# First loads in a fixed order and sixteen operand differences on GpSimd, in a two-layer encoder kernel

## The chip, the core and the metric

The kernel runs on one core of one Trainium2 chip. Its engines are TensorE (PE in the profile; PEld is its weight load), VectorE (DVE), ScalarE (ACT), GpSimd (POOL) and SyncE (SP). SP only issues DMAs; ACT issues a few beside its own work. The metric is the device time of one execution in microseconds, as a median of several runs.

## What is computed

A two-layer encoder trunk over two groups of 512 tokens of width 1024, with the same weights for both groups.

```python
def trunk(x, ...):
    for i in range(DEPTH):                       # DEPTH = 2
        h = rms_norm(x, norm_g[i], NORM_EPS)
        if i % N_MIXERS == 0:
            x = x + diff_attention(h, da_w_in[j], ..., da_w_out[j], lambda_init)
        else:
            x = x + bidir_retention(h, ret_w_in[j], ..., ret_w_out[j])
    return rms_norm(x, final_norm_g, NORM_EPS)

def diff_attention(h, w_in, ...):
    proj = h @ w_in                              # (512, 1024) @ (1024, 8192)
    q, k, v, gate = jnp.split(proj, ...)
    # rotary q and k, two softmaxes a head, their difference times v,
    # a norm a head, times silu(gate)
    return o @ w_out                             # (512, 2048) @ (2048, 1024)
```

The second layer has the same shape of projections (1024 to 6144 columns), with retention in both directions in place of the softmaxes. `reference` calls `trunk` once for `x_prompt` and once for `x_sample`.

## The kernel before

**Precision.** Each float32 operand of a large product is split into a high part, rounded to the matmul's fast float type, and a low part, the remainder. A product of two such operands takes three matmuls (`PASSES`). ACT makes the high part (`hi_of`, line 419), DVE the low part (`lo_of`, line 422), which reads the source and the high part and so two tensors of SBUF when the source lies there.

**Input projections.** They go by a scheme of seven products in place of eight for a two-by-two block of operands (the two groups of tokens on one side, halves of weight columns and of the inner dimension on the other). Per 256 weight columns there is a `Unit`; its seven products are called P1 to P7 and each needs one activation operand: B11, B21, T1, T2, B22, T3 and T4 (`B_OF`). These seven are made once per layer, in four pieces (k = 0 to 3) of 128 x 512 with a high and a low part, by `make_b` (line 467). It turns the normed tokens by transposes through PSUM, scales them by the norm's gain, and combines them: `h11` and `h21` are the first group's halves, `t` is first the second group's half less `h11` (T1) and then the other half less that (`scaled`, line 482; T2). The third piece's operand is `t - h11` (T3) and the fourth's `h21 - t` (T4). Both differences go through `sub` (line 494), one DVE `tensor_tensor` of 128 x 512, four for T3 and four for T4 in each layer; then `split` makes their high and low parts.

**Start.** Twenty short matmuls on zeros (`warm_up(10)`, line 1061) run first on PE. `x_norm` (line 1064) squares a row tile of 128 tokens on ACT, takes the root on POOL and scales the tile on ACT or DVE. For the first group the tiles are turned one at a time as they come (`turns`, line 1106), and `first_piece` (line 1089) makes B11's pieces in two halves of 256 tokens. `gains` (line 440) turns the norm gains, loaded as rows, into columns; it needs the identity matrix, as all transposes do. In the first two units P1 is issued in small steps: `prep` splits unit 0's first weight tile in four parts (lines 607 to 613), and `product` issues each of the two P1s as eight steps of three matmuls on 256 columns, by half and k (lines 650 to 661). All other products are one step of twelve matmuls on 512 columns (line 633).

**Order.** The program is not issued as it is written. Each operation is put into a `Plan` with its engine, an estimate of its time, and what it reads and writes. `Plan.arrange` then simulates the engines and DMA queues and lists the operations in the order in which it would start them: for PE close to the written order, for the other engines by how soon PE needs the result. It does so three times, each time with PE's simulated times from before, and the shortest list is issued. Each engine then works through its list in order. The planner knows no contention between DVE and POOL. `plan.first` (line 82), where it is set, makes every load that is put in afterwards wait, in the list, for one earlier operation to have been placed.

**Loads.** `dma` (line 412) issues on SP unless an engine is named. The identity (line 426), the three gain rows (line 438) and the first group's row tile 1 (line 1033) go on ACT's queue; the other row tiles and all weights on SP's.

Of the kernel before, what the change touches and what calls it, by code (L numbers as in the profile page):

```python
# [16 lines left out]
S = 512  # L17
# [238 lines left out]
def trunk_kernel(  # L256
# [167 lines left out]

    ident = const([P, P], "ident")
    dma(lambda: ident.t, lambda: ident_in, [], [ident], 64, nc.scalar)
    mhalf = const([P, NT], "mhalf")
    dve(4, lambda: nc.vector.memset(mhalf.t, -0.5), [], [mhalf])
    minus1 = const([P, 1], "minus1")
# [4 lines left out]
    for i, (lo, hi, src) in enumerate((  # L434
            (0, 16, norm_g.rearrange("l (k p) -> (l k) p", p=P)),
            (16, 18, da_subln_g.rearrange("l (k p) -> (l k) p", p=P)),
            (18, 20, ret_subln_g.rearrange("l (k p) -> (l k) p", p=P)))):
        dma(lambda lo=lo, hi=hi: rows[lo:hi, :], lambda src=src: src, [], [(rows, i)], 8, nc.scalar)

    def gains(behind):  # L440

# [25 lines left out]
    def make_b(layer, source):  # L467


        def parts(name, k, hi, lo, r):  # L470
            t = slot(B_SLOT[name] + k, [P, 2, S])
            hi(lambda: t[:, 0, :], r, [(t, 0)])
            lo(lambda: t[:, 1, :], lambda: t[:, 0, :], r + [(t, 0)], [(t, 1)])
            Bop[name, k] = t

        def split(name, k, src, key):
            parts(name, k, lambda out, r, w: hi_of(S, out, src, r, w),
                  lambda out, hi, r, w: lo_of(S, out, src, hi, r, w), [key])

        def scaled(out, ps, scale, less, r, w):  # L480

            dve(S, lambda: nc.vector.scalar_tensor_tensor(  # L482
                out(), ps.t, scale(), less(), op0=ALU.mult, op1=ALU.subtract), [ps, gcol] + r, w)

        def split_bank(name, k, ps, scale):
            parts(name, k, lambda out, r, w: plan.op(
                "ACT", 0.1 + 0.00092 * S,
                lambda: nc.scalar.activation(out(), ps.t, AF.Copy, scale=scale()), r + [gcol], w),
                lambda out, hi, r, w: scaled(out, ps, scale, lambda: hi().bitcast(F32), r[1:], w), [ps])

        def copy(out, ps, scale, late=()):
            evac(S, out[0], lambda: ps.t, scale, [ps, gcol, *late], [out[1]])

        def sub(out, a, b):

            dve(S, lambda: nc.vector.tensor_tensor(out[0](), a[0](), b[0](), op=ALU.subtract),
                [a[1], b[1]], [out[1]])

        def half(t, i):
            return (lambda: t[:, i, :]), (t, i)  # L500

        def whole(t):
            return (lambda: t.t), t

        two = [os_t(F32, "h") for _ in range(3)]
        h11 = [half(two[k // 2], k % 2) for k in range(4)]
        h21 = [whole(m_t("h")) for _ in range(4)]
        for name, h, k0 in (("B11", h11, 0), ("B21", h21, 4)):
            for k in range(4):
                if (name, k) in Bop and layer == 0:  # L510
                    for n in range(2):
                        ps, src = turned[n][k // 2], slice(k % 2 * 256, k % 2 * 256 + 256)
                        here = slice(n * 256, n * 256 + 256)
                        evac(256, lambda h=h[k][0], here=here: h()[:, here], lambda ps=ps, src=src: ps[:, src],
                             lambda k=k: gain(0, k), [ps, gcol, (Bop[name, k], (1, n))], [h[k][1]])
                    yield
                    continue
                bank_ = source(0, k0 + k)
                if layer == 0:
                    split_bank(name, k, *bank_)  # L520
                copy(h[k], *bank_, [(Bop[name, k], 1)] if layer == 0 else [])
                if not (layer == 0):
                    split(name, k, *h[k])
                yield
        t = [whole(e_t("h")), whole(e_t("h")), half(two[2], 0), half(two[2], 1)]
        for k in range(4):
            ps, scale = source(1, k)
            scaled(t[k][0], ps, scale, h11[k][0], [h11[k][1]], [t[k][1]])
            split("T1", k, *t[k])
            yield  # L530
        for k in range(4):
            ps, scale = source(1, 4 + k)
            scaled(t[k][0], ps, scale, t[k][0], [t[k][1]], [t[k][1]])
            split_bank("B22", k, ps, scale)
            split("T2", k, *t[k])
            sub(h11[k], t[k], h11[k])
            split("T3", k, *h11[k])
            yield
        for k in range(4):
            sub(h21[k], h21[k], t[k])  # L540
            split("T4", k, *h21[k])
            yield


    class Unit:
# [32 lines left out]
        def prep(self, op):  # L578
            x = self.take
            n = 256 if self.wide else P  # L580

            def combine(a, b, fn):
                t = st_t([P, 4, n])
                out = ((lambda: self.like(t.t)), t)
                dve(4 * n, lambda: nc.vector.tensor_tensor(out[0](), a[0](), b[0](), op=fn), [a[1], b[1]], [t])
                return out
            if op == "P1":
                src = x(0, 0)
            elif op == "P2":
                src = x(0, 1)  # L590
            elif op == "P4":
                src = x(1, 1)
            elif op == "P5":
                src = self.s[1] = combine(x(1, 0), x(1, 1), ALU.add)
            elif op == "P6":
                src = self.s[2] = combine(self.s[1], x(0, 0), ALU.subtract)
            elif op == "P3":
                src = combine(x(0, 1), self.s[2], ALU.subtract)
            else:
                src = combine(x(0, 0), x(1, 0), ALU.subtract)  # L600
            if self.wide:
                a, b = ws_t([P, 4, n], True), ws_t([P, 4, n], True)
                hi, lo = ((lambda: a.t), a), ((lambda: b.t), b)
            else:
                s = ws_t([P, 2, 4, n])
                hi, lo = ((lambda: s[:, 0]), (s, 0)), ((lambda: s[:, 1]), (s, 1))
            if op == "P1" and self is first_units[0]:
                for k in range(4):
                    hi_of(n, lambda k=k: self.like(hi[0]())[:, k], lambda k=k: src[0]()[:, k], [src[1]], [(s, (0, k))])
                    lo_of(n, lambda k=k: self.like(lo[0]())[:, k], lambda k=k: src[0]()[:, k],  # L610
                          lambda k=k: self.like(hi[0]())[:, k], [src[1], (s, (0, k))], [(s, (1, k))])
                self.ops[op] = (hi, lo)
                return
            hi_of(4 * n, lambda: self.like(hi[0]()), src[0], [src[1]], [hi[1]])
            lo_of(4 * n, lambda: self.like(lo[0]()), src[0], lambda: self.like(hi[0]()), [src[1], hi[1]], [lo[1]])
            self.ops[op] = (hi, lo)
            if op == "P2" and self.early is not None:
                self.early, self.x = None, {}

        def product(self, op):  # L620
# [27 lines left out]
            if not self.wide:  # L648
                ps = self.banks[which][0]
                if op == "P1" and self in first_units[:2]:  # L650
                    def piece(k, half):
                        here = slice(half * 256, half * 256 + 256)
                        for i, (u, v) in enumerate(PASSES):
                            nc.tensor.matmul(
                                ps[:, here], a[u][0]()[:, k, :], bt[k][:, v, here], start=(half + k + i == 0),
                                stop=(k == 3 and i == 2), skip_group_check=True)
                    for half in range(2):
                        for k in range(4):
                            pe(0.36, lambda k=k, half=half: piece(k, half),
                               ([(a[0][1][0], (n, k)) for n in range(2)] if self is first_units[0] else reads[:2])  # L660
                               + [(bt[k], (0, half)), (bt[k], (1, half))], [(ps, (k, half))])
                else:
                    pe(2.79, lambda: pair(ps), reads, [ps])
                return
# [365 lines left out]
    for g in range(NG):  # L1030
        for t in range(NT):
            x = xnat[g, t] = slot(20 + 4 * g + t, [P, D], F32)
            dma(lambda x=x: x.t, lambda g=g, t=t: xs[g][0, t * P:(t + 1) * P, :], [], [x], 512,
            nc.scalar if (g, t) == (0, 1) else None, 2.0 if g else 0.6)
            if g == 0:
                plan.first = len(plan.ops) - 1
        if g == 0:
# [566 lines left out]
```

## Time and profile before

| | |
|---|---|
| median of 3 runs | 1807.33 us (1807.0 to 1808.09) |
| profiled execution | 1806.59 us, span 1804.5 us |
| granted clock of TensorE, mean | 0.999 |
| DMA | 328.81 MB, mean 182 GB/s |
| ACT, of the span | 50% |
| POOL, of the span | 9%, x315 |

A line number in the profile is one of the kernel's; where a helper records an operation, it is the helper's (419 and 422 for all splits, 496 for all sixteen differences). `out<-in` gives the buffers: ws, raw and st hold weights, arena and b the activation operands, e, m, os and c are working buffers in SBUF, pad holds columns, and pj, sc, o and tp are banks of PSUM. The profiled execution's own time contains some 2.1 us around the span.

### The profile page before, as it was taken

What the parts mean: (1) busy time and instruction counts of PE and PEld (TensorE: products, weight loads), DVE (VectorE), ACT (ScalarE), POOL (GpSimd) and SP (SyncE); (2) the same over time, 40 slices, a digit from 0 to 9 for tenths busy, and PEclk for the clock granted to TensorE, in tenths of its full rate; (3) what the DMA queues carried; (4) which work ended last, traced back from release to release, by engine and by line L of the source; (5) the groups of instructions that cost most, each with busy time, mean ns of one, the idle gap of its engine ahead of it and who ended that gap; (6) DMA issues with size and microseconds to landing.
All of it is one profiled execution on the core that took longest, in us unless ns stands there. A gap on an engine that the chain in (4) does not pass through costs nothing.

```text
span 1804.5 us, 27874 instructions
## 1 busy us (share of the span) xinstructions
PE 1789.8 (99%) x10333; PEld 1566.1 (87%) x10333; DVE 1479.1 (82%) x2344; ACT 895.9 (50%) x1865; POOL 169.2 (9%) x315
## 2 busy tenths in 40 slices
PE   9999999999999999999999999999999999999998
PEld 7889889898988888888888888898989998888887
DVE  8967878778699888888888897787887967888887
ACT  8753344443343565555454866444444455444446
POOL 1000000000000022322322200000000000111113
PEclk9999999999999999999999999999999999999999
DMA  6444455655545594444554524464647459664652
GB/s 218 134 134 135 158 150 166 199 164 155 177 124 187 204 344 179 172 162 156 179 205 140 195 68 147 140 210 156 207 151 231 144 182 399 262 232 185 228 216 94
DMA packets 162767, 328.81 MB, mean 182 GB/s; under 512 B 12724, under 2 KB 76872, under 8 KB 162632
## 3 DMA queue, kind: packets, MB, share of 16 engines
q1 hardware_dynamic: 162160, 326.18, 53.5%
q8 instruction: 81, 1.33, 0.3%
q10 hardware_dynamic: 472, 0.86, 0.1%
q14 instruction: 54, 0.44, 0.1%
HBM read 209.55 MB, written 117.44 MB: 181 GB/s over the span
## 4 chain that ended last, share of the span: by engine, by line
PE 93%; DVE 3%; ACT 1%; DMA 1%; issue 0%; POOL 0%; SPq 0%; ACTq 0%; POOLq 0%; DVEq 0%
PE pj L633 20%; PE pj L934 19%; PE sc L633 11%; PE pj L643 10%; PE o L633 8%; PE o L1251 5%; PE sc L643 5%; PE sc L1186 5%; PE o L1429 2%; PE o L643 2%; PE tp L1231 1%; PE sc L1385 1%; PE tp L1409 1%; PE o L1437 1%; DVE ws L422 1%; DMA raw<-in_da_w_out_dram 1%
## 5 line engine op out<-in xcount | busy, mean ns | idle before, releaser
L934 PE MATMUL pj<-ws,arena 128*128 128x512 f32 x1542 | 389.8, 396 | 0.0
L934 PEld LDWEIGHTS pj<-ws,arena 128*128 128x128 f32 x1542 | 277.3, 188 | 50.6
L633 PE MATMUL pj<-b,ws 128*128 128x512 f32 x1080 | 263.2, 390 | 0.0
L633 PEld LDWEIGHTS pj<-b,ws 128*128 128x128 f32 x1080 | 201.3, 188 | 41.7 <-DVE e L687 0.5
L939 DVE SCALAR_TENSOR_TENSOR b<-pj,pad,b 128x512 f32<-128x512 f32 (+1 forms) x257 | 190.2, 744 | 23.0 <-PE pj L934 21.7
L422 DVE TENSOR_TENSOR ws<-st,ws 128x512 fp32r<-128x512 f32 (+1 forms) x192 | 147.9, 774 | 70.4 <-ACT ws L419 52.8
L422 DVE TENSOR_TENSOR ws<-raw,ws 128x512 fp32r<-128x512 f32 (+2 forms) x167 | 141.9, 855 | 69.4 <-ACT ws L419 59.5
L419 ACT CAST ws<-st 128x512 fp32r<-128x512 f32 (+1 forms) x192 | 132.0, 693 | 123.4 <-PE pj L633 34.6
L633 PE MATMUL sc<-arena,ws 128*128 128x512 f32 x768 | 185.2, 390 | 0.0
L633 PE MATMUL o<-arena,ws 128*128 128x512 f32 x744 | 178.4, 391 | 1.1 <-DVE arena L482 1.1
L633 PEld LDWEIGHTS sc<-arena,ws 128*128 128x128 f32 x768 | 143.9, 188 | 29.7
L419 ACT CAST ws<-raw 128x512 fp32r<-128x512 f32 (+2 forms) x167 | 126.2, 762 | 84.7 <-PE o L633 46.6
L633 PEld LDWEIGHTS o<-arena,ws 128*128 128x128 f32 x744 | 138.5, 188 | 30.3 <-DVE arena L482 2.0
L633 PE MATMUL pj<-arena,ws 128*128 128x512 f32 x624 | 153.1, 390 | 0.0
L633 PEld LDWEIGHTS pj<-arena,ws 128*128 128x128 f32 x624 | 116.4, 188 | 23.9
L1204 ACT ACTIVATE b<-sc,pad 128x512 f32<-128x512 f32 x128 | 87.9, 688 | 69.3 <-DVE pad L1194 68.5
L679 ACT COPY c<-pj 128x512 f32<-128x512 f32 x104 | 60.9, 586 | 115.2 <-PE pj L633 62.7
L643 PE MATMUL pj<-ws,b 128*128 128x256 f32 x960 | 116.9, 275 | 0.0
L643 PEld LDWEIGHTS pj<-ws,b 128*128 128x128 f32 x960 | 113.3, 188 | 0.6
L1186 PE MATMUL sc<-arena 128*128 128x512 f32 x384 | 99.6, 393 | 0.0
L1251 PEld LDWEIGHTS o<-arena 128*128 128x128 f32 x768 | 96.1, 189 | 3.3 <-ACT arena L419 0.7
L1251 PE MATMUL o<-arena 128*128 128x256 f32 x768 | 97.1, 284 | 0.5 <-ACT arena L419 0.5
(221 smaller groups left out, 2875.9 us busy)
## 6 DMA issues: line engine op xcount, KB each, us to landing
qk<-os SPq DMA_DIRECT2D x192, 256.0 KB, 3.4
arena<-qk SPq DMA_DIRECT2D x96, 512.0 KB, 5.9
raw<-in_da_w_in_dram SPq DMA_DIRECT2D x64, 512.0 KB, 4.8
v<-os SPq DMA_DIRECT2D x64, 512.0 KB, 3.7
arena<-v SPq DMA_DIRECT2D x64, 512.0 KB, 4.2
raw<-in_ret_w_in_dram SPq DMA_DIRECT2D x48, 512.0 KB, 4.4
os<-g SPq DMA_DIRECT2D x32, 512.0 KB, 8.1
g<-e SPq DMA_DIRECT2D x48, 256.0 KB, 4.6
```

The source lines that it names most:

```text
L419: act(n, lambda: nc.scalar.copy(dst(), src()), r, w)
L422: dve(n, lambda: nc.vector.tensor_tensor(dst(), src(), hi().bitcast(F32), op=ALU.subtract), r, w)
L633: nc.tensor.matmul(ps.t, a[u][0]()[:, k, :], bt[k][:, v, :], start=(opens and k == 0 and i == 0), stop=(k == 3 and i == 2), skip_group_che ...
L643: nc.tensor.matmul(ps[:, (t % 2) * 256:(t % 2) * 256 + 256], bt[k][:, v, t * P:(t + 1) * P], a[u][0]()[:, k, :], start=(opens and t % 2 == ...
L679: act(S, lambda c=c, ps=ps: nc.scalar.copy(c.t, ps.t), [ps], [c])
L934: nc.tensor.matmul(ps[:, here], o[a][:, e, t * P:(t + 1) * P], u[b][:, e, here], start=(m == 0), stop=(m == 5))
L939: axpy(n, lambda half=half, here=here, ps=ps: nc.vector.scalar_tensor_tensor(half, ps[:, here], rr[:, t % 2:t % 2 + 1], half, op0=ALU.mult ...
L1186: nc.tensor.matmul(s.t, q[:, a, t * P:(t + 1) * P], k[:, b, :], start=(n == 0), stop=(n == 2))
L1204: act(840, lambda j=j, s=s, m=m: nc.scalar.activation(p[:, j, :], s.t, AF.Exp, bias=m.t, accum_out=sm[:, 2 * j + n:2 * j + n + 1]), [s, m] ...
L1231: nc.tensor.transpose(tp[:, j * P:(j + 1) * P], p[:, 0, j * P:(j + 1) * P], ident.t)
L1251: nc.tensor.matmul(o[:, e * 256:(e + 1) * 256], v[b][:, j, e * P:(e + 1) * P], aT[a][:, j, :], start=(n == 0), stop=(n % 12 == 11), skip_g ...
L1429: nc.tensor.matmul(o[:, e * 256:(e + 1) * 256], v_[v][:, 2 * c + j, e * P:(e + 1) * P], a_[:, u, j * 256:(j + 1) * 256], start=(e == 0 and ...
```

## The change

Five edits:

- After the identity's load, `plan.first` is set to it until the three gain rows are in the plan, so that they are issued behind it.
- Row tile 1 of the first group is loaded on SP's queue like the others.
- `sub` puts its operation on POOL in place of DVE, in both layers (sixteen operations).
- Unit 0's first weight tile is split in two parts of 256 columns in place of four of 128, and P1's steps wait for the part that they use.
- Unit 1's P1 is issued as four steps of three matmuls on 512 columns, by k alone, in place of eight on 256.

```diff
@@ -424,6 +424,7 @@
     ident = const([P, P], "ident")
     dma(lambda: ident.t, lambda: ident_in, [], [ident], 64, nc.scalar)
+    plan.first = len(plan.ops) - 1
     mhalf = const([P, NT], "mhalf")
@@ -436,6 +437,7 @@
         dma(lambda lo=lo, hi=hi: rows[lo:hi, :], lambda src=src: src, [], [(rows, i)], 8, nc.scalar)
+    plan.first = None
@@ -493,8 +495,8 @@
         def sub(out, a, b):
 
-            dve(S, lambda: nc.vector.tensor_tensor(out[0](), a[0](), b[0](), op=ALU.subtract),
-                [a[1], b[1]], [out[1]])
+            pool(S, lambda: nc.gpsimd.tensor_tensor(out[0](), a[0](), b[0](), op=ALU.subtract),
+                 [a[1], b[1]], [out[1]])
@@ -605,10 +607,12 @@
             if op == "P1" and self is first_units[0]:
-                for k in range(4):
-                    hi_of(n, lambda k=k: self.like(hi[0]())[:, k], lambda k=k: src[0]()[:, k], [src[1]], [(s, (0, k))])
-                    lo_of(n, lambda k=k: self.like(lo[0]())[:, k], lambda k=k: src[0]()[:, k],
-                          lambda k=k: self.like(hi[0]())[:, k], [src[1], (s, (0, k))], [(s, (1, k))])
+                for k in range(2):
+                    ks = slice(2 * k, 2 * k + 2)
+                    hi_of(2 * n, lambda ks=ks: self.like(hi[0]())[:, ks], lambda ks=ks: src[0]()[:, ks], [src[1]],
+                          [(s, (0, k))])
+                    lo_of(2 * n, lambda ks=ks: self.like(lo[0]())[:, ks], lambda ks=ks: src[0]()[:, ks],
+                          lambda ks=ks: self.like(hi[0]())[:, ks], [src[1], (s, (0, k))], [(s, (1, k))])
                 self.ops[op] = (hi, lo)
                 return
@@ -654,10 +658,14 @@
+                    if self is first_units[1]:
+                        for k in range(4):
+                            pe(0.7, lambda k=k: pair(ps, (k,)), reads[:2] + [bt[k]], [(ps, k)])
+                        return
                     for half in range(2):
                         for k in range(4):
                             pe(0.36, lambda k=k, half=half: piece(k, half),
-                               ([(a[0][1][0], (n, k)) for n in range(2)] if self is first_units[0] else reads[:2])
+                               ([(a[0][1][0], (n, k // 2)) for n in range(2)] if self is first_units[0] else reads[:2])
                                + [(bt[k], (0, half)), (bt[k], (1, half))], [(ps, (k, half))])
@@ -1031,7 +1039,7 @@
             dma(lambda x=x: x.t, lambda g=g, t=t: xs[g][0, t * P:(t + 1) * P, :], [], [x], 512,
-            nc.scalar if (g, t) == (0, 1) else None, 2.0 if g else 0.6)
+            None, 2.0 if g else 0.6)
```

## Prediction

> **What bounds the kernel now.** I read the page first, for the engines' shares.
>
> ```profile
> span 1804.5 us, 27874 instructions
> PE 1789.8 (99%) x10333; PEld 1566.1 (87%) x10333; DVE 1479.1 (82%) x2344; ACT 895.9 (50%) x1865; POOL 169.2 (9%) x315
> ```
>
> TensorE (PE) is busy 99% of the span, and VectorE (DVE) 82%. So a faster DVE is worth something only where PE waits for it. Where that is, the chain that ended last tells; I read it in time order, for the first 110 us and for the stretch around 1050 us, where the second layer begins. Columns: start, length, what.
>
> ```profile
> 1.64 7.17 DMA ident<-in_ident_dram
> ...
> 9.52 0.88 DVE b L406 x2
> ...
> 49.27 0.67 DVE arena L482
> ...
> 49.99 5.73 PE o L633 x24
> ...
> 1053.63 0.67 DVE arena L482
> ...
> 1054.35 3.02 PE o L633 x12
> ```
>
> The chain begins with the load of the identity matrix, goes over to DVE at about 9 us, stays on it until 49.95, and is then PE's own work until the end of the first layer. At the second layer's start DVE carries it again, up to 1054.3. Everything else of the kernel is PE work in its own rate. How much PE really loses in these two places is in the busy time by windows (window, length, then busy time and count of PE, PEld, DVE, ACT, POOL; the clock; DMA share; GB/s):
>
> ```profile
> 40.00:50.00 10.00, 7.90 (x42) 5.98 (x40) 10.00 (x17) 7.45 (x13) 0.00 (x0) 1.00 0.01 2
> 50.00:80.00 30.00, 30.00 (x132) 24.88 (x133) 30.00 (x51) 20.99 (x36) 0.00 (x0) 1.00 0.39 118
> ...
> 1050.00:1060.00 10.00, 9.03 (x43) 7.06 (x43) 10.00 (x17) 7.44 (x13) 0.00 (x0) 1.00 0.00 1
> 1060.00:1080.00 20.00, 20.00 (x90) 16.57 (x89) 20.00 (x34) 13.73 (x24) 0.00 (x0) 1.00 0.41 132
> ```
>
> PE idles 10.00 - 7.90 = 2.1 us in the first and 10.00 - 9.03 = 0.97 us in the second. From 50 to 80 and from 1060 to 1080 it idles not at all, although DVE is full there. POOL does nothing in any of the four. The clock is 1.00 throughout.
>
> **The loads at the start.** The timeline and the waits of the first 15 us:
>
> ```profile
> 1.17 0.44 ACTq L415 DMA_DIRECT2D b<-in_x_prompt_dram  x1
> 1.17 6.86 PE L1059 MATMUL sc<-e 128*128 128x256 f32 x20 [1.17 <-DVE pad L430]
> 4.33 1.06 ACT L1068 ACTIVATE arena<-b 128x1024 fp32r<-128x1024 f32 x1
> 7.52 1.06 ACT L1068 ACTIVATE arena<-b 128x1024 fp32r<-128x1024 f32 x1 [2.05 <-DMA b<-in_x_prompt_dram]
> 8.91 0.20 PE L443 MATMUL pj<-ident,m 20*128 20x20 f32 x1 [0.89 <-DMA ident<-in_ident_dram]
> 10.23 1.04 ACT L1068 ACTIVATE arena<-b 128x1024 fp32r<-128x1024 f32 x1
> ...
> 14.02 0.36 PE L654 MATMUL pj<-arena,ws 128*128 128x256 f32 x1
> ```
>
> ```profile
> 5.00:10.00 5.00, 4.12 (x19) 3.06 (x18) 1.64 (x9) 2.95 (x6) 1.08 (x2) 1.00 1.04 390
> ```
>
> Row tile 1 travels on ScalarE's (ACT's) queue while tiles 0, 2, 3 travel on SP's; ACT, which takes the tiles in turn, waits 2.05 us for it and squares it at 7.52. The identity is behind that tile on the same queue, and the first transpose waits until 8.91. After the change the four tiles come in turn. At 390 GB/s a tile of 524 kB takes 1.34 us; tile 0 is there at 4.33 at the latest, so tile 1 follows at 5.67 and tile 3 at 8.35, which is 7.52 - 5.67 = 1.85 us and 10.23 - 8.35 = 1.88 us sooner. The identity, 64 kB at the head of its queue, comes before tile 1.
>
> But PE's queue is in order, and ahead of the first transpose stand the twenty warm-up matmuls, which end at 1.17 + 6.86 = 8.03. So the gains' transpose (L443), the turning of tiles 0 and 1 behind it, and the DVE copies that wait for both, move forward by 8.91 - 8.03 = 0.88 us and no more, however early the identity is. DVE's chain from there to 49.95 consists of its own work back to back, so what its beginning gains, its end gains. Bounds: 1.9 us sooner, if DVE can use the earlier tiles 2 and 3 as well, and 0.4 us later, if one more issue (0.44 us) ahead of tiles 2 and 3 on SP shows. I take **-0.9 us**, as the warm-ups' end lies on the way of all that follows. What moves past what: SP issues four tiles in a row in place of three, ACT issues one DMA fewer, and the three gain rows stand behind the identity; their first user is L443, covered by the same warm-ups.
>
> **The pieces of the first two products.** Rows of the splits and of the matmuls:
>
> ```profile
> L422 DVE TENSOR_TENSOR ws<-raw,ws x7: 276/281/681, 13.4 to 23.2; 128x128 fp32r<-128x128 f32 x4, 128x512 fp32r<-128x512 f32 x3
> ```
>
> ```profile
> 18.13 3.87 PE L654 MATMUL pj<-arena,ws 128*128 128x256 f32 x30
> ...
> 19.18 0.47 DVE L1097 SCALAR_TENSOR_TENSOR arena<-o,pad,arena 128x256 fp32r<-128x256 f32 x1
> ```
>
> Four low parts of 128 columns at 0.28 us become two of 256. Between 0.28 (128) and 0.68 (512) a line gives 0.28 + 128 x 0.40 / 384 = 0.41, so DVE goes from 1.12 to 0.82 us; the first piece comes 0.13 us later and the second sooner. Bounds: -0.3 to +0.13 us; I take nothing, since neither exceeds what DVE's order may shuffle.
>
> Unit 1's 24 matmuls of 256 columns (3.87 / 30 = 0.129 us each, 3.1 us) become 12 of 512 (30.00 / 132 = 0.227 us, 2.7 us): 0.4 us less of PE. It is worth nothing as long as DVE's chain decides at 49.99. The price would be the wait for the second halves of the four activation pieces. The last low half is done at 19.18 + 0.47 = 19.65, while unit 1's 24 are the last of the thirty and start at 18.13 + 6 x 0.129 = 18.9; its fourth piece comes two microseconds later than that, so it does not wait. Bounds: -0.4 to +0.75 (if all of it waited for 19.65); I take 0.
>
> **The sixteen differences.** Eight per layer. First layer, where they stand and what needs them:
>
> ```profile
> 42.24 0.74 DVE L482 SCALAR_TENSOR_TENSOR e<-tp,pad,e 128x512 f32<-128x512 f32 x1
> ...
> 56.54 1.28 DVE L496 TENSOR_TENSOR os<-e,os 128x512 f32<-128x512 f32 x2
> ...
> 59.55 2.48 DVE L422 TENSOR_TENSOR b<-os,b 128x512 fp32r<-128x512 f32 x4
> ...
> 66.44 5.60 PE L633 MATMUL pj<-b,ws 128*128 128x512 f32 x24
> ...
> 69.17 2.49 DVE L422 TENSOR_TENSOR b<-m,b 128x512 fp32r<-128x512 f32 x4
> ...
> 74.60 4.24 PE L633 MATMUL pj<-b,ws 128*128 128x512 f32 x18
> ```
>
> Two take 1.28 us, and consecutive ones stand 0.60 apart, so DVE is relieved of 8 x 0.60 = 4.8 us in each layer. But the first stands at 56.54, behind the last DVE step of the chain (49.27), in a stretch where PE has no gap. So this relief buys nothing directly: 0 us. On POOL eight take, by the seven of the same shape there,
>
> ```profile
> L1475 POOL TENSOR_TENSOR e<-b,cos x7: 1296/1301/1589, 1775.8 to 1794.7; 128x512 f32<-128x512 f32 x7
> ```
>
> 8 x 1.30 = 10.4 us. The first one's operands are complete at 42.24 + 0.74 = 42.98 us, and POOL is idle there, so four can be done by about 50 us and eight by about 56, when DVE now only starts them; the splits of the third pieces end 4.4 us ahead of their product (62.03 to 66.44) and those of the fourth 2.9 us ahead (71.66 to 74.60). POOL's slowness is covered; without that cover it would be 1.30 - 0.60 = 0.7 us for each.
>
> What is not covered is that both engines read SBUF. The trace shows one side of it:
>
> ```profile
> 8.94 0.55 POOL L1070 TENSOR_TENSOR pad<-pad,pad 128x1 f32<-128x1 f32 x1 [2.66 <-DVE pad L1069]
> ...
> 25.12 0.68 DVE L585 TENSOR_TENSOR st<-st,raw 128x512 f32<-128x512 f32 x1
> ```
>
> ```profile
> 24.68 1.53 POOL pad L1070
> ```
>
> ```profile
> 1775.52 0.68 DVE L422 TENSOR_TENSOR arena<-c,arena 128x512 fp32r<-128x512 f32 x1
> 1775.77 1.59 POOL L1475 TENSOR_TENSOR e<-b,cos 128x512 f32<-128x512 f32 x1
> ```
>
> The same POOL operation takes 0.55 us elsewhere and 1.53 us while DVE runs operations with two SBUF tensors, whose durations stay at 0.68; the 512-column one that met such an operation is the 1.59 among the 1.30. So POOL yields, and DVE pays nothing. The other order, a two-tensor DVE operation that finds a long POOL operation under way, no row shows. Its cost per difference lies between -0.60 us (the relief, if DVE's slot there counted) and 1.30 us (DVE held for all of it). I take 0, by the rows above, which are the nearest.
>
> The Trainium skill speaks against this. "SBUF — State Buffer", section "Who interferes with whom", says that a DVE instruction with two SBUF inputs contends with a GpSimd instruction that reads SBUF, and that whichever comes first has the shared pair for its whole length. For POOL's waits the rows agree; by the rule DVE would be held too, which is the slower rival.
>
> **Sum.** -0.9 + 0 + 0 + 0 = -0.9 us on the profiled execution, whose own time is 1806.59 (the span of 1804.5 and 2.1 around it): 1805.7. The median of the runs, 1807.33, is 0.74 above that execution, so **1806.4 us**, with a range of its own of 1805.4 (-1.9) to 1807.7 (+0.4).
>
> **Rivals.**
>
> *DVE held by POOL: slower.* Place: the two stretches before PE resumes. From the moment the first differences are ready, DVE has these two-tensor operations ahead of PE's restarts, five in the first layer and two in the second (first and last of each):
>
> ```profile
> 43.56 0.67 DVE L422 TENSOR_TENSOR ws<-st,ws 128x512 fp32r<-128x512 f32 x1
> ...
> 48.60 0.67 DVE L585 TENSOR_TENSOR st<-raw,st 128x512 f32<-128x512 f32 x1
> ...
> 1051.70 0.68 DVE L422 TENSOR_TENSOR ws<-st,ws 128x512 fp32r<-128x512 f32 x1
> ...
> 1052.96 0.68 DVE L422 TENSOR_TENSOR b<-e,b 128x512 fp32r<-128x512 f32 x1
> ```
>
> A POOL difference that starts beside a one-tensor operation (L482, 0.67) holds the next two-tensor one for 1.30 - 0.67 = 0.63; one that slips in between two such holds 1.30. Three of the five follow a one-tensor operation, two follow each other: 3 x 0.63 + 2 x 1.30 = 4.5 us; in the second layer 2 x 0.63 = 1.3. With the start that is -0.9 + 4.5 + 1.3 = +4.9: **1812.2 us**. It decides from 4.5 us of holding on, where it passes the gain at the start by 3.6. For it: the case of 1.59 shows that the two do exclude each other. Against: where they met, DVE was never longer. Chance 0.30. A milder form, where POOL gets in only beside one-tensor operations: 5 x 0.63 = 3.2, hence +2.3, 1809.6; chance 0.10.
>
> *PE's gaps close: faster.* If the new order of DVE, with eight operations fewer, lets the steps that PE waits for go first, the 2.1 and 0.97 us of idle time go, and the tiles' full 1.85 at the start: -4.9, **1802.4 us**. For it: the gaps are DVE's. Against: the differences stand behind the gaps, so their absence frees no slot ahead of them. Chance 0.26.
>
> **How the numbers follow.** The forecast, 1806.4, has chance 0.34, the held DVE 0.30, its milder form 0.10, the closed gaps 0.26. About 0.2%, 3.6 us, is what a measurement of this kernel can tell from no change; so faster (below 1803.7) 0.26, same 0.34 + 0.10 = 0.44, slower (above 1810.9) 0.30. The range reaches from 1801, which leaves out some 0.06 of the closed gaps, to 1813, which leaves out the worst of the held DVE, some 0.12.
>
> **What would show it.** Tile 1 squared at about 5.7 and the gains' transpose at about 8.1 confirm the start; a transpose at 8.9 refutes it. The chain should hand over from DVE to PE at about 49.1 and 1053.4. The differences on POOL should last 1.3 us, or more where DVE reads two tensors. Two-tensor DVE operations longer than 0.68, or pauses ahead of them while POOL runs, and PE restarts after 51 and 1055 us, would prove the slower rival. The forecast is wrong if PE waits for a third or fourth operand piece, or if DVE in its new order starts a needed split later than now.

## The result and the profile after

The changed kernel takes 1813.11 us (median of 6 runs, 1812.03 to 1817.25) beside 1807.34 us for the kernel before (6 runs, 1806.56 to 1808.3): 1.0035 times as long, 95% interval 1.0025 to 1.0046. It is 5.8 us slower, where 0.9 us faster was forecast. The profiled execution took 1812.03 us, 5.44 more than that of before.

The head of the page, as first in the prediction:

```profile
span 1810.1 us, 27853 instructions
PE 1791.2 (99%) x10321; PEld 1566.0 (87%) x10321; DVE 1478.9 (82%) x2325; ACT 895.0 (49%) x1864; POOL 193.3 (11%) x331
```

Sixteen differences have left DVE and two splits of weights have gone, yet its busy time is the same to 0.2 us (1479.1 before). POOL has 24.1 us more. The windows of the two stretches show where the time is (window, length, then busy time and count of PE, PEld, DVE, ACT, POOL; clock, DMA share, GB/s):

```profile
40.00:50.00 10.00, 7.60 (x31) 5.76 (x29) 10.00 (x13) 7.91 (x15) 8.14 (x6) 0.83 0.01 2
50.00:80.00 30.00, 29.62 (x131) 24.24 (x130) 29.97 (x48) 19.57 (x35) 4.58 (x3) 1.00 0.43 132
...
1050.00:1060.00 10.00, 7.93 (x42) 6.25 (x42) 10.00 (x14) 7.66 (x14) 6.73 (x5) 1.00 0.07 28
1060.00:1080.00 20.00, 17.50 (x78) 14.15 (x77) 20.00 (x29) 13.52 (x25) 6.05 (x4) 1.00 0.31 106
```

The column to read is DVE's: it is as full as before, but in 40 to 50 us it does 13 operations in place of 17, in 1050 to 1060 14 in place of 17, in 1060 to 1080 29 in place of 34. PE idles 2.40 + 0.38 us in the first two windows (before 2.10 + 0) and 2.07 + 2.50 us in the last two (before 0.97 + 0). The clock, 1.00 in all of them before, is 0.83 in the first. The timelines of DVE and of POOL in that window (start, length, operation):

```profile
42.03 1.40 DVE L587 TENSOR_TENSOR st<-st,raw 128x512 f32<-128x512 f32 x1
43.35 0.74 DVE L484 SCALAR_TENSOR_TENSOR arena<-tp,pad,arena 128x512 fp32r<-128x512 f32 x1
44.01 1.10 DVE L422 TENSOR_TENSOR ws<-st,ws 128x512 fp32r<-128x512 f32 x1
...
47.01 3.02 DVE L422 TENSOR_TENSOR b<-e,b 128x512 fp32r<-128x512 f32 x2
49.95 0.74 DVE L484 SCALAR_TENSOR_TENSOR arena<-o,pad,arena 128x512 fp32r<-128x512 f32 x1
```

```profile
41.60 2.97 POOL L498 TENSOR_TENSOR os<-e,os 128x512 f32<-128x512 f32 x2 [12.21 <-ACT c L789]
44.52 1.72 POOL L498 TENSOR_TENSOR m<-m,e 128x512 f32<-128x512 f32 x1
46.51 2.97 POOL L498 TENSOR_TENSOR os<-os,os 128x512 f32<-128x512 f32 x2 [0.26 <-DVE os L484]
```

Every DVE operation here that reads two tensors of SBUF is long: 1.40, 1.10, and 3.02 for a pair of splits, where before one took 0.68 and a pair 1.28. L484, which reads one operand from PSUM, keeps its 0.74 although POOL works beside it. The long ones end just behind a POOL difference: POOL's first pair is over at 41.60 + 2.97 = 44.57, and the split of 44.01 ends at 45.11, 0.54 later; the second pair is over at 46.51 + 2.97 = 49.48, and DVE's pair of splits at 47.01 + 3.02 = 50.03, 0.55 later. So each waits until the difference that it finds under way is done, and then takes some 0.55 us of its own. Fourteen DVE operations of the two stretches are lengthened like this, and every one of them ends 0.54 to 0.56 us behind the end of a difference. By the timelines they last 19.3 us together; 14 x 0.68 = 9.5, so DVE was held for 9.8 us. The relief was 16 x 0.60 = 9.6. That is why DVE's busy time has not changed. The chain of waits shows what it does to PE:

```profile
42.11 1.23 DVE st L587
...
47.09 2.94 DVE b L422 x2
50.03 0.67 DVE arena L484
50.75 5.74 PE o L637 x24
...
1055.51 1.03 DVE b L422
...
1059.71 1.78 DVE arena L422
...
1064.90 1.70 DVE ws L422
...
1070.19 0.69 DVE e L695
1070.93 3.03 PE o L637 x12
```

In the first layer DVE hands over to PE at 50.75 instead of 49.99. In the second the chain of before leaves DVE at 1054.35; now it stays there until 1070.93, because DVE is held further behind the first restart. PE's rows with what ended the idle time ahead of them:

```profile
45.83 4.54 PE L637 MATMUL o<-arena,ws 128*128 128x512 f32 x12 [0.59 <-DVE arena L484]
...
1070.93 1.42 PE L637 MATMUL o<-arena,ws 128*128 128x512 f32 x5 [2.50 <-DVE e L695]
```

The second row is the new wait of 2.50 us (the view ends at 1072, so only five of the twelve matmuls are in it). The first is the clock: twelve matmuls in 4.54 us, where twelve of the same form take 3.03 at 1070.93. A mean clock of 0.83 over 10 us is (1 - 0.83) x 10 / 0.5 = 3.4 us at half rate (the window from 46 to 49 us alone shows 0.50); it followed pauses of PE of 1.81 us, which ended at 44.14, and of 0.59, which ended at 45.83. So PE lost 0.30 + 0.38 + 1.51 = 2.2 us more than before in the first layer (had the clock stayed up, the 1.51 would have been idle time, since the restart at 50.75 waits for DVE) and 1.10 + 2.50 = 3.6 us in the second: 5.8 us, as much as the medians differ by (the profiled executions differ by 5.4). What the start gained, some 1.1 us, and what more PE paused between 600 and 700 us, 0.8 us by the windows, about cancel; both are taken up with e1 at the end.

### The profile page after: what moved, and what is told of

Same layout as the page of the kernel before. It is cut to its first block, busy times and chain, and to the rows that moved or that the text cites. A ratio compares the mean times of both kernels' runs of the same rounds, so it can differ in the third digit from the quotient of the medians.

```text
span 1810.1 us, 27853 instructions
## 1 busy us (share of the span) xinstructions
PE 1791.2 (99%) x10321; PEld 1566.0 (87%) x10321; DVE 1478.9 (82%) x2325; ACT 895.0 (49%) x1864; POOL 193.3 (11%) x331
## 4 chain that ended last, share of the span: by engine, by line
PE 93%; DVE 4%; ACT 2%; DMA 1%; issue 1%; POOL 0%; SPq 0%; POOLq 0%; DVEq 0%; ACTq 0%
PE pj L637 20%; PE pj L942 19%; PE sc L637 10%; PE pj L647 10%; PE o L637 8%; PE o L1259 5%; PE sc L647 5%; PE sc L1194 4%; PE o L1437 2%; PE o L647 2%; PE tp L1239 1%; PE sc L1393 1%; PE tp L1417 1%; PE o L1445 1%; DVE ws L422 1%; DMA raw<-in_da_w_out_dram 1%
## 5 line engine op out<-in xcount | busy, mean ns | idle before, releaser
L1212 ACT ACTIVATE b<-sc,pad 128x512 f32<-128x512 f32 x128 | 87.9, 688 | 69.3 <-DVE pad L1202 68.5
```

The lines of the kernel that those rows point to most:

```text
L1212: act(840, lambda j=j, s=s, m=m: nc.scalar.activation(p[:, j, :], s.t, AF.Exp, bias=m.t, accum_out=sm[:, 2 * j + n:2 * j + n + 1]), [s, m] ...
```

## The experiments

Each edit is against the changed kernel, unless it says otherwise; ratios are against the kernel before on the same chip, whose median there was 1806.76 to 1806.87 us.

### The differences back on DVE, alone on POOL, and in one layer only

`e1_sub_dve` keeps the loads and the pieces and takes the differences back:

```diff
-            pool(S, lambda: nc.gpsimd.tensor_tensor(out[0](), a[0](), b[0](), op=ALU.subtract),
+            dve(S, lambda: nc.vector.tensor_tensor(out[0](), a[0](), b[0](), op=ALU.subtract),
```

> The changed kernel with the sixteen differences back on DVE; the loads and the first pieces as changed. Held theory (a difference on POOL holds DVE's operations with two SBUF tensors): the loss is gone and the start's gain stays, 8.91 - 7.44 = 1.5 us at the first transpose, so about 1806 us, and no operation of DVE at 43 to 52 us above 0.74 us. Start theory (the loads or the first pieces cost the time): still above 1810 us.

`e2_only_sub` is the kernel before with only this edit, the other way round:

```diff
-            dve(S, lambda: nc.vector.tensor_tensor(out[0](), a[0](), b[0](), op=ALU.subtract),
+            pool(S, lambda: nc.gpsimd.tensor_tensor(out[0](), a[0](), b[0](), op=ALU.subtract),
```

> The kernel before with only the sixteen differences moved to POOL. Held theory: the whole loss without the start's gain, 1813.1 + 1.5 = about 1814.5 us; PE resumes after 52 us in the first layer. Start theory: 1807.3 us.

`e4_sub_first` has the differences on POOL in the first layer, `e5_sub_second` in the second (there with `layer == 1`):

```diff
+            if layer == 0:
+                pool(S, lambda: nc.gpsimd.tensor_tensor(out[0](), a[0](), b[0](), op=ALU.subtract),
+                     [a[1], b[1]], [out[1]])
+                return
+            dve(S, lambda: nc.vector.tensor_tensor(out[0](), a[0](), b[0](), op=ALU.subtract),
+                [a[1], b[1]], [out[1]])
```

> The changed kernel with the differences on POOL in the first layer alone. If each layer's loss is its own: PE's idle time grows by 2.2 us at 40 to 60 us as in the changed kernel (5.08 against 2.92 with all on DVE), and by nothing in the second layer: 1805.6 + 2.2 = about 1807.8 us. If the loss is made in one layer alone, either 1805.6 or 1813.

> The changed kernel with the differences on POOL in the second layer alone. PE's idle time there grew by 2.64 - 1.55 + 2.77 = 3.9 us: 1805.6 + 3.9 = about 1809.5 us. If the loss is made in the first layer alone: 1805.6 us.

| kernel | median, us | ratio to before, 95% |
|---|---|---|
| e1, differences on DVE | 1805.62 | 0.9992 [0.9983, 1.0001] |
| e2, only the differences on POOL | 1813.46 | 1.0038 [1.0024, 1.0051] |
| e4, POOL in the first layer | 1808.62 | 1.0013 [1.0004, 1.0023] |
| e5, POOL in the second layer | 1810.79 | 1.0022 [1.0012, 1.0031] |

The differences alone bring the whole loss (e2), and without them it is gone (e1). In e2 the chain hands over to PE at 52.38, after 52 as expected. The chain of waits of e1 hands over to PE in the first layer and at the second layer's first restart, as before, and the last window has no idle time of PE:

```profile
47.60 0.60 DVE arena L422
48.20 0.67 DVE arena L484
48.92 5.74 PE o L637 x24
...
1054.30 3.02 PE o L637 x12
```

```profile
1060.00:1080.00 20.00, 20.00 (x90) 16.57 (x89) 20.00 (x34) 13.71 (x24) 0.00 (x0) 1.00 0.42 132
```

Against its own kernel before, e1 stands at -1.1 us, e4 at +1.8 and e5 at +4.0. So the first layer costs 2.9 us and the second 5.1, together 8.1, more than the 6.9 of both at once. PE's row in e5 and the window around it show the surplus:

```profile
1069.05 4.46 PE L641 MATMUL o<-arena,ws 128*128 128x512 f32 x12 [2.48 <-DVE e L699]
```

```profile
1070.00:1074.00 4.00, 4.00 (x13) 3.10 (x12) 4.00 (x8) 2.34 (x5) 0.00 (x0) 0.57 0.65 196
```

The same wait of 2.5 us as in the changed kernel, but here the clock fell behind it, and twelve matmuls took 4.46 us in place of 3.03: 1.4 us. In the changed kernel's profile the clock stayed up behind this wait. e5's ten times fall into two groups of five, 1809.4 to 1810.4 and 1811.2 to 1811.6, some 1.4 us apart, and the profiled execution is one of the longer; so a clock that falls in half of the executions would put some 0.7 us of it into the median, of the 1.2 that the sum has too much. Only one execution was profiled, so this is not shown. e4 and e5 took 0.8 and 1.3 us more than expected.

### Is it POOL's length, its reads or its writes?

`e3_short_sub` shortens each difference to 4 of its 512 columns.

```diff
-            pool(S, lambda: nc.gpsimd.tensor_tensor(out[0](), a[0](), b[0](), op=ALU.subtract),
+            pool(S, lambda: nc.gpsimd.tensor_tensor(out[0]()[:, 0:4], a[0]()[:, 0:4], b[0]()[:, 0:4], op=ALU.subtract),
```

> The changed kernel with each difference on POOL taken over 4 of its 512 columns (the third and fourth operand pieces keep the old values in the rest). The order on PE, DVE, ACT and POOL is that of the changed kernel. Held theory: DVE's two-tensor operations are back at 0.68 us each, and the time is 1806 to 1808 us. Order theory (the planner's new order alone loses the time, because it puts DVE's operations in a worse sequence): 1812 to 1814 us, as the changed kernel.

1806.48 us, ratio 0.9999 [0.999, 1.0008]. On every engine the instructions stand in the same order as in the changed kernel, with the same waits, and only the length of the sixteen differs. DVE's timeline, the operations that were long above:

```profile
44.06 0.68 DVE L587 TENSOR_TENSOR st<-st,raw 128x512 f32<-128x512 f32 x1
...
47.89 1.27 DVE L422 TENSOR_TENSOR b<-e,b 128x512 fp32r<-128x512 f32 x2
```

They are back at 0.68 and at 1.27 for the pair. The order and the waits of the new program are not the loss; how long POOL works beside DVE is.

`e6_memset` fills the result with zeros in place of the difference, and `e11_memset_place` computes one column and fills the other 511.

```diff
-            pool(S, lambda: nc.gpsimd.tensor_tensor(out[0](), a[0](), b[0](), op=ALU.subtract),
-                 [a[1], b[1]], [out[1]])
+            pool(S, lambda: nc.gpsimd.memset(out[0](), 0.0), [a[1], b[1]], [out[1]])
```

> The changed kernel with a memset of the same 128 x 512 tile on POOL in place of each difference (the third and fourth operand pieces become zero). POOL writes as much but reads nothing from SBUF. If it is the read side that the engines share, DVE's two-tensor operations stay at 0.68 us and the time is 1806 to 1808 us. If any long POOL operation on SBUF holds DVE, they are as long as in the changed kernel for the part that the memset lasts, and the time lies between 1808 and 1813 us.

```diff
+            def fn():
+                nc.gpsimd.tensor_tensor(out[0]()[:, 0:1], a[0]()[:, 0:1], b[0]()[:, 0:1], op=ALU.subtract)
+                nc.gpsimd.memset(out[0]()[:, 1:], 0.0)
+            pool(S, fn, [a[1], b[1]], [out[1]])
```

> The changed kernel with each difference replaced by a difference of one column and a memset of the other 511 behind it, so that the memset runs where the difference ran (the third and fourth operand pieces become zero but for a column). Read theory: a write alone holds nothing, DVE's operations stay at 0.68 to 0.74 us, 1805.5 to 1807.5 us. If any POOL operation on SBUF holds DVE: two-tensor operations beside the memsets of 0.9 us and more, above 1808 us.

e6 took 1807.17 us, ratio 1.0001 [0.9991, 1.001], but says little: with no operand to read, the fills ran at 36 to 42 us, ahead of most of the DVE operations in question. e11 puts them in their place: 1806.08 us, 0.9994 [0.9985, 1.0003]. POOL's and DVE's timelines of e11:

```profile
43.48 0.53 POOL L500 MEMSET os<- 128x511 f32 x1
...
50.64 3.79 POOL L499 TENSOR_TENSOR m<-m,os 128x1 f32<-128x1 f32 x1
```

```profile
43.78 0.69 DVE L589 TENSOR_TENSOR st<-st,raw 128x512 f32<-128x512 f32 x1
...
54.28 0.76 DVE L484 SCALAR_TENSOR_TENSOR arena<-tp,pad,arena 128x512 fp32r<-128x512 f32 x1
```

The first of DVE's two-tensor operations runs beside the fill in 0.69 us, unheld, and of the 21 that ran beside POOL's work in the two layers none took more than 0.70. A POOL operation that only writes did not hold DVE. The 3.79 us are the reverse case: one column of POOL work waited while DVE ran operation after operation with two tensors, until 54.43, when DVE had come to L484 at 54.28, which reads one.

`e10_one_input` copies the first operand (times 1.0), which reads one tensor.

```diff
-            pool(S, lambda: nc.gpsimd.tensor_tensor(out[0](), a[0](), b[0](), op=ALU.subtract),
+            pool(S, lambda: nc.gpsimd.tensor_scalar(out[0](), a[0](), 1.0, None, op0=ALU.mult),
```

> The changed kernel with each difference on POOL replaced by a copy of its first operand (one SBUF input in place of two; the third and fourth operand pieces lose their second operand), in the same order on every engine. Held theory (the two engines share one read path): DVE's two-tensor operations are still held, for as long as the shorter copy lasts. If it takes 0.6 to 0.7 us, half of the changed kernel's loss, 1808 to 1811 us. If only two inputs on POOL hold DVE: no operation of DVE above 0.74 us, and 1805.5 to 1807.

1807.21 us, ratio 0.9998 [0.9989, 1.0007]. POOL's and DVE's timelines of e10:

```profile
46.60 1.49 POOL L498 TENSOR_SCALAR m<-m 128x512 f32<-128x512 f32 x1
```

```profile
45.41 0.89 DVE L422 TENSOR_TENSOR ws<-st,ws 128x512 fp32r<-128x512 f32 x1
```

The copies are nearly as long as the differences (1.49 to 1.66 us against 1.28 to 1.76), so length alone does not do it either. The split that met one took 0.89, which is 0.2 over; of 21 operations with two tensors the median is 0.69 and the longest 1.09. Neither expectation is met exactly: a copy holds DVE, but for a part of its time. By these runs it is the difference, with two reads, that holds DVE to its end. The copy is also another kind of instruction, and no run separates that from the number of reads.

The Trainium skill's "SBUF — State Buffer", section "Who interferes with whom", which the prediction weighed, also says that a GpSimd instruction which only writes does not contend; the 0.69 of e11 agrees. It makes no distinction between one read and two on GpSimd's side, which the 0.89 of e10 beside the 1.40 of the changed kernel shows here.

### Is it the place ahead of PE's restarts, or the amount?

`e9_later` holds each layer's differences until the low part of B22's last piece is made (by a small POOL operation that reads it), so that they fall behind the first restart. The prediction had seen no gap of PE there, so by place alone the loss should vanish; by amount it should stay.

```diff
+            if "gate" not in held:
+                held["gate"] = col(1, f"gate{layer}", 1)
+                t = Bop["B22", 3]
+                pool(1, lambda: nc.gpsimd.tensor_tensor(
+                    held["gate"].t, t[:, 1, 0:1].bitcast(F32), t[:, 1, 1:2].bitcast(F32), op=ALU.add), [(t, 1)], [held["gate"]])
...
-                 [a[1], b[1]], [out[1]])
+                 [a[1], b[1], held["gate"]], [out[1]])
...
             split("T2", k, *t[k])
+            yield
+        for k in range(4):
             sub(h11[k], t[k], h11[k])
             split("T3", k, *h11[k])
-            yield
```

> The changed kernel, with POOL kept from its differences until the low part of the last piece of B22 is made (one small POOL operation reads it ahead of them), so that they run after PE has resumed. Place theory (DVE held matters only ahead of PE's restart; behind it the 4.8 us of relief in each layer pay for it): PE resumes as early as with all on DVE, 48.9 and 1054.3 us, and the time is 1805.5 to 1807 us, though DVE's two-tensor operations are held there too. Amount theory (each held operation costs, wherever it stands): 1811 to 1814 us.

1820.55 us, ratio 1.0077 [1.0062, 1.0092]: worse than the change itself and outside both expectations. Timelines of DVE, POOL and PE, and a window of e9:

```profile
51.70 1.78 DVE L595 TENSOR_TENSOR st<-raw,st 128x512 f32<-128x512 f32 x1
53.40 1.77 DVE L422 TENSOR_TENSOR ws<-st,ws 128x512 fp32r<-128x512 f32 x1
```

```profile
52.88 3.43 POOL L505 TENSOR_TENSOR os<-os,os 128x512 f32<-128x512 f32 x2
```

```profile
49.76 5.74 PE L645 MATMUL o<-arena,ws 128*128 128x512 f32 x24 [0.75 <-DVE arena L484]
...
1077.64 5.49 PE L645 MATMUL o<-arena,ws 128*128 128x512 f32 x12 [5.59 <-DVE e L703]
```

```profile
60.00:100.00 40.00, 35.45 (x152) 27.68 (x151) 36.27 (x58) 27.31 (x48) 3.12 (x2) 1.00 0.48 154
```

PE's first restart, 49.76, is unharmed. But here DVE has hardly anything except operations with two tensors, and the two engines take turns: the second DVE operation starts 1.70 us after the first (51.70, 53.40), and each POOL difference takes 3.43 / 2 = 1.7. So a difference costs DVE 1.70 - 0.60 = 1.10 us where it relieves it of 0.60, and DVE's busy time is 1485.9 us, 7.0 above the changed kernel's. PE runs out of work later: 4.55 us idle in 60 to 100, where it had none before, and 5.59 us ahead of 1077.64, with 5.49 - 3.03 = 2.5 us more at half clock behind that. These three come to 12.6 us beside the 13.7 lost. Amount decides, and the place sets the amount, by what DVE runs there: DVE was full, and "no gap of PE" was not spare time of DVE. In the changed kernel the balance is even, since one-tensor operations like L484 run beside a part of POOL's work.

### The start

`e7_loads` is the kernel before with the two edits to the loads alone:

```diff
+    plan.first = len(plan.ops) - 1
...
+    plan.first = None
...
-            nc.scalar if (g, t) == (0, 1) else None, 2.0 if g else 0.6)
+            None, 2.0 if g else 0.6)
```

> The kernel before with only the loads changed (identity ahead of the gain rows, row tile 1 on SP's queue). If the loads make the start's gain: 0.9 to 1.5 us below before, 1805.5 to 1806.3 us, and the first transpose follows the last warm-up at once. If the pieces of the first products make it: as before, 1806.8 us.

`e8_warm` is e1 with fourteen warm-up matmuls in place of twenty, as the prediction had named their end as the bound:

```diff
-    warm_up(10)
+    warm_up(7)
```

> The differences on DVE, loads and pieces as changed, and 7 warm-up calls in place of 10. If the warm-ups' end bounds the start, the first transpose moves from 7.4 to 8.6 us forward to the last gain row's or tile 0's arrival, about 6.5 to 7 us, and the time falls by up to 1 us below all of them with 10: 1804.5 us. If DVE and ACT bound the start (row tile 3 comes at 8.4 us whatever PE does): 1805.6 us, as with 10. If the clock needs the warm-ups: above 1806.

e7 took 1805.94 us, 0.9996 [0.9987, 1.0006]; e8 1806.25 us, 0.9995 [0.9986, 1.0004]. With e1 at 0.9992 all three are 0.6 to 1.1 us below the kernel before, and none is clear of it. PE's timeline of the changed kernel, of e1 and of e8, first to last:

```profile
1.17 6.34 PE L1067 MATMUL sc<-e 128*128 128x256 f32 x20 [1.17 <-DVE pad L431]
7.44 0.23 PE L445 MATMUL pj<-ident,m 20*128 20x20 f32 x1
```

```profile
8.62 0.23 PE L445 MATMUL pj<-ident,m 20*128 20x20 f32 x1
```

```profile
1.17 5.51 PE L1067 MATMUL sc<-e 128*128 128x256 f32 x14 [1.17 <-DVE pad L431]
6.67 0.20 PE L445 MATMUL pj<-ident,m 20*128 20x20 f32 x1
```

The transpose follows the warm-ups at once in each, as foreseen. But their end is not the same from run to run (7.44 and 8.62 for the same twenty), and e8, with its transpose 1.95 us ahead of e1's, hands over to PE as good as together with it. Its chain of waits, and the second layer's restart:

```profile
5.01 5.82 DMA raw<-in_da_w_in_dram
...
48.81 5.73 PE o L637 x24
...
1053.21 3.02 PE o L637 x12
```

That is 0.11 us before e1's 48.92. In e1, where the warm-ups end late, they are on the chain. In e8 the chain begins with loads instead: the first weights land at 5.01 + 5.82 = 10.83, and ACT's split of them comes next. So these weights bound the start just as closely as the warm-ups do. In e7's profile the chain goes through the same load, which lands there at 11.24.

## Why the prediction was wrong

**The step that failed** is in "The sixteen differences": "So POOL yields, and DVE pays nothing", and with it the zero for contention. The rows behind it were true (1.53 against 0.55, 1.59 against 1.30, DVE at 0.68), but they were a POOL operation on one column and one difference that came after a DVE operation. They show who waits when DVE comes first. The case the change makes, a DVE operation that finds a long POOL operation with two reads under way, was said to be in no row, and was then priced by the rows for the opposite order, at nothing. Measured, it is 9.8 us of holding for sixteen differences, 0.61 each, well inside the bounds of -0.60 to 1.30. e3 takes the holding away with the order kept, and the time goes from 5.8 us above the kernel before to 0.3 below. The sentence of the Trainium skill that the prediction cites, that whoever comes first keeps the pair for its whole length, is borne out by the ends 0.54 and 0.55 us behind POOL's.

**The slower rival** ("DVE held by POOL", 1812.2 us, chance 0.30) is what happened, at 1813.1. Its mechanism was right and its sizes by layer were not. It gave 4.5 us to the first layer and 1.3 to the second; PE lost 2.2 and 3.6. In the first layer four operations were held ahead of the hand-over, not five: 1.40 + 1.10 + 3.02 - 4 x 0.68 = 2.8 us, and one split that stands ahead of it in e1 (47.60) now stands behind it, which takes 0.6 off; DVE also came to the first held operation 0.45 us earlier than in e1 (42.03 against 42.48). So the hand-over moved by 50.75 - 48.92 = 1.8 us. In the second the count stopped at the first restart, 1054.35, while DVE was held on to 1066.6 and PE waited for it at 1070.93.

**The relief** was worth nothing by the sum of the prediction, and the medians agree: e3, which has the relief and no holding, is not faster than e1, which has neither (1806.48 against 1805.62). In its profile, that of the slowest of its ten executions (1807.69), DVE hands over to PE at 49.89, no sooner than before. PE is busy 9.29 us of the window 40 to 50 (7.90 before), which looks like a piece of the faster rival. But it idles 2.41 us between 10 and 20 (1.05 before), where 1.72 us go into a wait for ACT's split of weights, and so comes later to the place where it waits for DVE. Both windows together have 3.12 us of idle time, and 3.15 before: it has moved, and none has gone. The first line is before's, the others e3's:

```profile
10.00:20.00 10.00, 8.95 (x66) 7.75 (x66) 9.97 (x28) 10.00 (x25) 1.08 (x2) 1.00 1.06 384
```

```profile
10.00:20.00 10.00, 7.59 (x46) 6.90 (x46) 7.80 (x20) 7.71 (x18) 0.54 (x1) 0.83 1.04 377
...
40.00:50.00 10.00, 9.29 (x48) 7.06 (x47) 10.00 (x17) 8.06 (x15) 2.69 (x8) 1.00 0.07 28
```

But "a stretch where PE has no gap" hid that DVE is full there: e9 shows that more DVE work in it does cost.

**POOL's slowness is covered** was right where it was used: PE never waited for a difference itself. But the differences took up to 1.76 us (columns: shortest, median and longest of four, in ns), since POOL waits for DVE in its turn:

```profile
L498 POOL TENSOR_TENSOR os<-os,os x4: 1282/1515/1758, 46.5 to 1059.2; 128x512 f32<-128x512 f32 x4
```

**The start, -0.9 us,** was right in size as far as the runs can tell: -0.9 (e7) to -1.1 (e1), with intervals that include zero. That the size fits is luck in part: it was worked out from the warm-ups' end as the one bound, and e8 moves that end without moving the hand-over, as the first weights bound the start too. Tile 1 was squared at 5.86 (5.67 was worked out):

```profile
5.86 1.06 ACT L1076 ACTIVATE arena<-b 128x1024 fp32r<-128x1024 f32 x1 [0.19 <-DMA b<-in_x_prompt_dram]
```

e1 handed over to PE at 48.92, 1.07 us sooner than before (49.1 was foreseen). But at the second layer it was at 1054.30, level with before: between 600 and 700 us PE is busy 98.69 us in e1 and 99.44 before. It waits there 0.58 us for ACT (L1212) and 0.22 for DVE (L695), two waits that the profile of before does not have; why they arise stays open. The chain of e7, which has the loads alone, shows no gain even in the first layer, but that is the profile of one of its slowest executions (1807.11):

```profile
49.95 5.74 PE o L635 x24
```

Only e8's profile, that of the fastest of its executions (1804.87), shows a gain that lasts: there PE is busy 99.42 us between 600 and 700, and resumes the second layer at 1053.21. For the loads and pieces as changed there is the 1 us of the medians and no more.

**The pieces** at nothing: no run separates them from the loads by more than the 0.3 us between e1 and e7.

## What to carry to other kernels

Before moving an elementwise operation with two SBUF operands from DVE to POOL, count what DVE runs beside it: here each such POOL operation held the two-tensor operation that found it under way to its own end (up to 1.1 us, for a relief of 0.6), while operations that read one of their tensors from PSUM passed (0.74). A stretch in which PE never waits is no proof that the engine feeding it has time to spare; look at that engine's own busy time. And a row for A waiting on B is not a price for B waiting on A: when the trace lacks the order that the change makes, carry both bounds into the sum.

## What the runs showed of the hardware beside this

The granted clock fell to half for 3.4 us behind pauses of PE of some 2 us: 0.57 over four microseconds in e5, behind 2.48 us, which is (1 - 0.57) x 4 / 0.5 = 3.4 us at half rate, but not in the changed kernel behind 2.50 us at the same place (its window there shows 1.00). The Trainium skill, "TensorE: Matmul & The Clock Gate", section "Part 1: The HAM clock gate", has a window of 3.4 us that runs by itself and a half rate after an idle one; the length and the rate agree. Chance by the window's phase would fit the two cases, though their pauses are shorter than a window, and no run here shows the phase. The one pause here that is longer, 5.59 us in e9, ended at 1077.64, and the clock was 0.50 from 1077 to 1083 us.

A short POOL operation can wait for long: one column took 3.79 us in e11 while DVE ran two-tensor operations back to back, yet full differences took strict turns with DVE in e9 (1.70 us apart). What decides between the two stays open.
